# Input weights in chunks of 512 rows instead of 256, and the combined output weights made earlier in a tile that then holds the low-rank products

## The chip, the cores and the metric

The kernel runs on one core of one Trainium2 chip. The metric is device time in microseconds, the median of several runs. A difference under about 0.2% (4 us) is not told from no difference.

## What is computed

One step of one layer of a hybrid decoder, in float32: 1024 prompt rows with 16 learned rows ahead of them, and 32 rows of 8 sampled sequences, 2048 wide.

```python
u = h @ w_in                      # h: rms-normed rows; 2048 -> 7184 columns
sq, sk, sv, sg, gq, gk, gv, gg, ga = jnp.split(u, idx, axis=-1)
log_f = jax.nn.log_sigmoid(ga @ w_alpha + b_alpha) / GLA_TAU      # ga: 16 columns
o_sb  = stick_breaking_attention(sq, sk, sv)      # 8 heads of 128, the sampled rows with paged k and v
o_gla = gated_linear_attention(gq, gk, gv, log_f) # 4 heads, 128 keys, 256 values
mixed = jnp.concatenate([o_sb * silu(sg), rms_norm(o_gla) * silu(gg)], axis=-1)
y = x + rms_norm(mixed @ w_out)
```

## The kernel before

All matrix products are made in three passes of a fast float format: a factor is split into a high part (a cast) and a low part (what the cast lost), and high x high, high x low and low x high are summed in PSUM. `hT` holds the normed rows, transposed: 16 tiles of 128 columns, each with the high part (`hh`) and the low part (`hl`) of 1072 rows. It is made at the start: the rows come as nine tiles x0 to x8 (two halves each, `load_x`), are squared on ScalarE (L224), scaled on VectorE (L235), transposed on TensorE (L259) in three thirds of the rows, and evicted by ScalarE (L260, times `gpre`, the high part) and VectorE (L261, the low part). Meanwhile TensorE makes the first projection, v of head 0, from the tiles `wf` and `wfl` (L271 to L273). Some small constants are loaded beside it (L140 to L144); `nbal` (a row for the gated part, L141) is negated by VectorE (L142).

A projection to 128 columns is `inproj` (L278): 16 blocks of 128 weight rows, in each three groups of rows (c = 0, 1, 2) with three passes, summed in three PSUM banks `acc`; a following projection takes the same three banks, one after another. The weights come through `weight_chunk` (L176): one DMA of 256 rows x 128 columns into `wr`, a cast by ScalarE to `wh` (L183), a subtraction by VectorE to `wl` (L184). The pool `wp` has three buffers of each, and the next chunk's load, cast and subtraction wait for a buffer. There are 56 projections of 8 chunks: v, k and q of eight heads, gates 0 to 2, then four heads of gated linear attention (k, q, two v each) with gates 3 and 4, and the other gates beside the sampled rows' part and the output.

The order of the work is written by hand: TensorE's loop calls `W.beat()` after each group of six matmuls of `inproj`, and generators that were given to the Weaver run at their beats and issue work for the other engines: `z_feed` (L386) multiplies the paged keys `kp` with the sampled queries `qb` on VectorE (four operations `jk` for each of 512 pages), the loads of the cached values `vr` and their split into `V` (L487, L488), `attend`, `gate_rest` for each gate (L418), and `weight_forms` (L401). Within an engine, work runs in the order in which it was placed; `urgent()` places it ahead. SP issues nearly all DMAs.

`weight_forms` makes sums and differences of the four quarters of `w_out` for the output stage: 16 tiles `tf`, each with four loads (L407), four subtractions on VectorE (L411) and four writes to DRAM (`td`, L414). There is one buffer `tf`, so a tile's loads wait for the writes of the one before. A tile takes 4 x 4 + 12 + 4 x 4 + 4 x 4 = 60 beats, and the generator starts at beat 10. The eight heads and gates 0 to 2 have 24 beats for each projection, 640 with the low-rank product, which stands between the heads and the gates (beats 552 to 568).

The low-rank product (`low_rank`, L313) is the projection to the 16 columns `ga`; it is evicted to a tile `ga` of its own (L328 to L330) and used by `decay` (L730) for each of the four gated heads. At the end of a head, q is evicted from PSUM by ScalarE (L624) and VectorE (L625, the low part, also from PSUM).

A gate's columns are copied from PSUM by ScalarE (`gx`, L442); `gate_rest` then alternates between VectorE (L426, L429, L431, L432) and ScalarE (L427, L428, L430), with a tile `go` read back from DRAM for L432. For a gated head, `level` makes X on VectorE (L780, L781), its exponential on ScalarE (L782); k and q are evicted by ScalarE in pieces (L672 to L680).

In the output stage, tiles of `w_out` and of the combined weights go through `ring` (cast L1308, subtraction L1309, 512 columns each) to the matmuls L1471 to L1473; `raw()` gives the tiles `fr` in which the mixed rows are loaded.

## Time and profile before

| | |
|---|---|
| median of 3 runs | 2113.27 us (2111.09 to 2113.43) |
| the profiled execution | 2108.24 us, of which the span in the trace is 2106.5 us |
| TensorE busy | 2056.2 us, 12,546 matmuls, mean granted clock 0.995 |
| VectorE busy | 1569.7 us |
| ScalarE busy | 991.8 us |
| DMA | 301.96 MB, mean 143 GB/s |

All times of instructions below are those of the profiled execution, counted from the start of its span. Its end lies 1.7 us before the execution's, and the execution is 5.0 us faster than the median; a sum of changes is made against 2108.24. The rows of the waits name who waited, for whom, how long in total, how often, and the longest. In a row of the timeline the start and the length come first, then engine, line, operation, output and inputs, and in brackets how long the engine had stood and for what. In a row of the groups the busy time of the group and the mean of one in ns follow the first bar, the idle time ahead of them and its cause the second.

### The profile page before, as it was taken

The page shows a single profiled execution, that of the slowest core. Times are in us where ns is not written, and L with a number is a line of the kernel's source. Part 1 is how long each engine was busy: PE and PEld are TensorE (multiplying, and loading weights), DVE is VectorE, ACT ScalarE, POOL GpSimd, SP SyncE. Part 2 cuts the span into 40 slices and gives each one's busy share as a digit, 9 for nine tenths or more (in the row PEclk, how much of TensorE's full clock was granted, in tenths as well). Part 3 has the DMA queues.
Part 4 walks back from the last instruction along what each step waited for, and adds up shares of the span by engine and source line. Part 5 has one row for each costly group of instructions (what it writes and reads, how often), then busy time and mean ns, then how long its engine had stood idle before and what let it go on. Part 6 is the DMA issues. An engine that isn't in the chain of part 4 may idle for free.

```text
span 2106.5 us, 43298 instructions
## 1 busy us (share of the span) xinstructions
PE 2056.2 (98%) x12546; PEld 1868.4 (89%) x12546; DVE 1569.7 (75%) x6593; ACT 991.8 (47%) x2539; POOL 80.9 (4%) x298
## 2 busy tenths in 40 slices
PE   5999999999999999999999999999999999999998
PEld 4999999999999989999899898998888888777776
DVE  6368888889888889899889988877544347453576
ACT  7346555565655547423535335353444326332342
POOL 0000000100000000020000000000000000000000
PEclk9999999999999999999999999999999999999999
DMA  6234443544444353544353444434776666352485
GB/s 200 72 103 123 132 131 100 144 118 121 139 124 126 108 145 102 156 132 117 110 138 104 123 129 113 107 85 135 244 234 219 224 218 201 127 159 75 130 279 186
DMA packets 378505, 301.96 MB, mean 143 GB/s; under 512 B 50073, under 2 KB 318777, under 8 KB 378265
## 3 DMA queue, kind: packets, MB, share of 16 engines
q1 hardware_dynamic: 376072, 298.91, 48.1%
q8 instruction: 99, 1.62, 0.3%
q14 instruction: 142, 1.16, 0.2%
q10 hardware_dynamic: 2192, 0.27, 0.1%
HBM read 241.75 MB, written 57.31 MB: 142 GB/s over the span
## 4 chain that ended last, share of the span: by engine, by line
PE 84%; DMA 6%; DVE 6%; ACT 2%; issue 1%; SPq 0%; DVEq 0%; POOL 0%; ACTq 0%; POOLq 0%
PE acc_g L288 4%; PE acc_g L290 4%; PE b L1471 4%; PE acc_g L289 4%; PE b L1472 4%; PE b L1473 4%; PE acc_k L288 3%; PE acc_gv L288 3%; PE acc_k L289 3%; PE acc_q L288 3%; PE acc_k L290 3%; PE acc_gv L290 3%; PE acc_gv L289 3%; PE acc_q L289 3%; PE acc_q L290 3%; PE acc_v L288 3%
## 5 line engine op out<-in xcount | busy, mean ns | idle before, releaser
L386 DVE SCALAR_TENSOR_TENSOR jk<-kp,qb 128x128 f32<-128x128 f32 x2048 | 591.6, 289 | 38.9 <-DMA qb<-qsd 1.5
L288 PE MATMUL acc_g<-hT,wh_g 128*128 128x368 f32 (+2 forms) x768 | 251.7, 328 | 0.8 <-ACT gx L442 0.8
L290 PE MATMUL acc_g<-hT,wl_g 128*128 128x368 f32 (+2 forms) x768 | 248.4, 323 | 0.0
L289 PE MATMUL acc_g<-hT,wh_g 128*128 128x368 f32 (+2 forms) x768 | 247.9, 323 | 0.0
L1471 PE MATMUL b<-ring,f 128*128 128x512 f32 x416 | 165.7, 400 | 3.2 <-ACT b L1344 2.0
L386 DVE DVE_READ_ACCUMULATOR jk<-kp,qb 128x1 f32 x2048 | 166.9, 81 | 0.0
L1309 DVE TENSOR_TENSOR ring<-wr,ring 128x512 fp32r<-128x512 f32 x104 | 70.6, 690 | 128.7 <-ACT ring L1308 128.3
L1472 PE MATMUL b<-ring,f 128*128 128x512 f32 x416 | 162.8, 391 | 0.7 <-DVE ring L1309 0.5
L1473 PE MATMUL b<-ring,f 128*128 128x512 f32 x416 | 162.4, 390 | 0.0
L288 PEld LDWEIGHTS acc_g<-hT,wh_g 128*128 128x128 f32 x768 | 145.1, 189 | 12.4 <-issue 10.2
L290 PEld LDWEIGHTS acc_g<-hT,wl_g 128*128 128x128 f32 x768 | 144.9, 189 | 2.0 <-issue 2.0
L289 PEld LDWEIGHTS acc_g<-hT,wh_g 128*128 128x128 f32 x768 | 145.1, 189 | 0.7
L1308 ACT CAST ring<-wr 128x512 fp32r<-128x512 f32 x104 | 64.4, 622 | 159.0 <-DMA wr<-in_w_out_dram 80.6
L288 PE MATMUL acc_gv<-hT,wh_gv 128*128 128x384 f32 (+1 forms) x384 | 129.6, 338 | 0.0
L288 PE MATMUL acc_k<-hT,wh_k 128*128 128x378 f32 (+1 forms) x384 | 127.8, 333 | 0.0
L288 PE MATMUL acc_q<-hT,wh_q 128*128 128x368 f32 (+2 forms) x384 | 125.5, 327 | 0.0
L289 PE MATMUL acc_k<-hT,wh_k 128*128 128x378 f32 (+1 forms) x384 | 125.5, 327 | 0.0
L290 PE MATMUL acc_k<-hT,wl_k 128*128 128x378 f32 (+1 forms) x384 | 125.3, 326 | 0.0
L290 PE MATMUL acc_gv<-hT,wl_gv 128*128 128x384 f32 (+1 forms) x384 | 125.2, 326 | 0.0
L289 PE MATMUL acc_gv<-hT,wh_gv 128*128 128x384 f32 (+1 forms) x384 | 124.6, 325 | 0.0
L289 PE MATMUL acc_q<-hT,wh_q 128*128 128x368 f32 (+2 forms) x384 | 123.8, 322 | 0.0
L290 PE MATMUL acc_q<-hT,wl_q 128*128 128x368 f32 (+2 forms) x384 | 123.6, 322 | 0.0
(441 smaller groups left out, 5398.3 us busy)
## 6 DMA issues: line engine op xcount, KB each, us to landing
kp<-in_cache_k_dram SPq DMA_DIRECT2D x512, 64.0 KB
vr<-in_cache_v_dram SPq DMA_DIRECT2D x64, 512.0 KB
tf<-in_w_out_dram SPq DMA_DIRECT2D x64, 256.0 KB
qb<-qsd SPq DMA_DIRECT2D x64, 256.0 KB
td<-tf SPq DMA_DIRECT2D x64, 256.0 KB
wr_g<-in_w_in_dram SPq DMA_DIRECT2D x128, 128.0 KB
wr<-td SPq DMA_DIRECT2D x64, 256.0 KB
wr<-in_w_out_dram SPq DMA_DIRECT2D x48, 256.0 KB
```

Source lines behind the costliest of these rows:

```text
L288: mm(acc[c][:, :n], wh[:, k2, :], hh[k][:, lo:hi], start=(k == 0), stop=False)
L289: mm(acc[c][:, :n], wh[:, k2, :], hl[k][:, lo:hi], start=False, stop=False)
L290: W.mark = mm(acc[c][:, :n], wl[:, k2, :], hh[k][:, lo:hi], start=False, stop=(k == NK - 1)).ins
L386: ins = vec.scalar_tensor_tensor(jk[:], kp[:], 1.0, qbs[h, b][:, t, :], ALU.mult, ALU.mult, accum_out=zt[:, t, NPG - 1 - i:NPG - i])
L1308: act.copy(wh, r)
L1309: vec.tensor_tensor(wl, r, wh.bitcast(F32), ALU.subtract)
L1471: mm(bk[:], ah, wh, start=first and k == 0, stop=False, skip_group_check=True)
L1472: mm(bk[:], ah, wl, start=False, stop=False, skip_group_check=True)
L1473: mm(bk[:], al, wh, start=False, stop=last and k == 7, skip_group_check=True)
```

## The change

- A weight chunk is 512 rows (four blocks of 128, one DMA of 256 KB), in two buffers instead of three: 224 loads, casts and subtractions instead of 448. The first projection's own tiles hold three chunks (12 blocks in `wf`, six pairs in `wfl`), the fourth uses the pool.
- `weight_forms` pauses half as long: 2 beats between its steps and 8 behind the loads, 32 beats for a tile instead of 60. It now ends at beat 522 instead of 970.
- The tile of the low-rank products is no longer one of its own. When `weight_forms` has ended, it takes the buffer `tf` under the name `ga`; `low_rank` runs beats until it is there (beat 522 lies ahead of its 552).
- The tiles `fr` of the output stage come from another pool, `op`, which is opened later and lies where the weights lay.

```diff
-    wp_cm = tc.tile_pool(name="wp", bufs=3, side="right")
+    wp_cm = tc.tile_pool(name="wp", bufs=2, side="right")
...
     def weight_chunk(w, kk, c0, nm, dst=None):
         with urgent():
-            raw = wp.tile([P, 2, P], F32, tag="wr", name=f"wr_{nm}")
-            nc.sync.dma_start(raw[:], w[kk * 256:(kk + 1) * 256, c0:c0 + P].rearrange("(k p) c -> p k c", p=P))
+            raw = wp.tile([P, 4, P], F32, tag="wr", name=f"wr_{nm}")
+            nc.sync.dma_start(raw[:], w[kk * 512:(kk + 1) * 512, c0:c0 + P].rearrange("(k p) c -> p k c", p=P))
+            wh, wl = dst or [wp.tile([P, 4, P], F32R, tag=t, name=f"{t}_{nm}") for t in ("wh", "wl")]
...
-        wf = xp.tile([P, 14, P], F32R, tag="wf", bufs=1, name="wf")
+        wf = xp.tile([P, 12, P], F32R, tag="wf", bufs=1, name="wf")
...
         for kk in range(NK // 2):
-            wh, wl = weight_chunk(w_in[0], kk, c0, f"{nm}_{kk}")
+            if kk % 2 == 0:
+                ws = weight_chunk(w_in[0], kk // 2, c0, f"{nm}_{kk // 2}")
...
-    ga = dk.tile([96, T], F32R, tag="ga", bufs=1, name="ga")
...
+        while not ga:
+            W.beat()
+        g = ga[0]
...
                 spread(nc.sync.dma_start(t[:, i, :], w_out[0, r0:r0 + P, c0:c0 + 512]))
-                yield 4
-            yield 12
+                yield 2
+            yield 8
             for i, a, b in ((0, 1, 0), (1, 1, 2), (2, 2, 0), (3, 3, 2)):
                 spread(vec.tensor_tensor(t[:, i, :], t[:, a, :], t[:, b, :], ALU.subtract))
-                yield 4
+                yield 2
             for j, i in enumerate((0, 2, 1, 3)):
                 spread(nc.sync.dma_start(td[j][:, k, q * 512:(q + 1) * 512], t[:, i, :]))
-                yield 4
+                yield 2
+        ga.append(dk.tile([96, T], F32R, tag="tf", bufs=1, name="ga"))
...
-            return oy.tile([P, 512], F32, tag="fr", name=nm)
+            return op.tile([P, 512], F32, tag="fr", bufs=4, name=nm)
```

What this does to the order shows at three places. In the rows, a name's last number only tells tiles apart; line numbers of the changed kernel are up to 8 higher.

**The start.** SP's loads from x3 on (the two halves of x3 are `x_0_232` and `x_1_233` before, `x_0_218` and `x_1_219` now; the next two are x4's). Before:

```order
L211 DMA x_0_232<-in_x_prompt_dram 128x1024
L179 DMA wr_v_1_202<-in_w_in_dram 128x2x128
L179 DMA wr_v_2_206<-in_w_in_dram 128x2x128
L211 DMA x_1_233<-in_x_prompt_dram 128x1024
L211 DMA x_0_236<-in_x_prompt_dram 128x1024
L179 DMA wr_v_3_210<-in_w_in_dram 128x2x128
```

and now:

```order
L214 DMA x_0_218<-in_x_prompt_dram 128x1024
L179 DMA wr_v_1_202<-in_w_in_dram 128x4x128
L214 DMA x_1_219<-in_x_prompt_dram 128x1024
L214 DMA x_0_222<-in_x_prompt_dram 128x1024
L179 DMA wr_v_2_207<-in_w_in_dram 128x4x128
L179 DMA wr_v_3_212<-in_w_in_dram 128x4x128
```

The second half of x3 stood behind two loads of weights after the first, and now stands behind one; it was the fourteenth DMA of the program, counting ScalarE's, and is now the thirteenth, with x4's first half as the fourteenth. Further down SP issued the constants behind the last rows and two chunks for head 0's k. Before:

```order
L179 DMA wr_k_1_917<-in_w_in_dram 128x2x128
L179 DMA wr_k_2_941<-in_w_in_dram 128x2x128
L140 DMA biasb<-in_sb_bias_dram 128x8
L211 DMA x_0_496<-in_x_prompt_dram 128x1024
L211 DMA x_1_497<-in_x_prompt_dram 128x1024
L209 DMA x_0_500<-in_x_sample_dram 32x1024 x2
L179 DMA wr_k_3_989<-in_w_in_dram 128x2x128
L179 DMA wr_k_4_1015<-in_w_in_dram 128x2x128
L141 DMA nbal<-in_b_alpha_dram 128x4x1
L143 DMA gnrm<-in_gla_norm_g_dram 128x2x1
```

and now:

```order
L214 DMA x_1_479<-in_x_prompt_dram 128x1024
L179 DMA wr_k_1_920<-in_w_in_dram 128x4x128
L179 DMA wr_k_2_989<-in_w_in_dram 128x4x128
L140 DMA biasb<-in_sb_bias_dram 128x8
L141 DMA nbal<-in_b_alpha_dram 128x4x1
L143 DMA gnrm<-in_gla_norm_g_dram 128x2x1
L214 DMA x_0_482<-in_x_prompt_dram 128x1024
L214 DMA x_1_483<-in_x_prompt_dram 128x1024
L212 DMA x_0_486<-in_x_sample_dram 32x1024 x2
```

`nbal` and `gnrm` have moved ahead of x7 (`x_0_496` before, `x_0_482` now) and x8. On VectorE the negation of `nbal` (L142) stood between x6's sums and the first hT of the second third. Before:

```order
L235 TENSOR_SCALAR x_0_373<-x_0_373,r_x_403 128x1024
L235 TENSOR_SCALAR x_1_374<-x_1_374,r_x_403 128x1024
L226 TENSOR_REDUCE sq_529<-ssq_524 128x1
L161 TENSOR_SCALAR v_x_531<-sq_529 128x1
L142 TENSOR_SCALAR nbal<-nbal 128x4
L261 SCALAR_TENSOR_TENSOR hT_146<-tx_0_506,gpre,hT_146 128x384
L261 SCALAR_TENSOR_TENSOR hT_147<-tx_1_512,gpre,hT_147 128x384
```

and now:

```order
L238 TENSOR_SCALAR x_0_222<-x_0_222,r_x_330 128x1024
L238 TENSOR_SCALAR x_1_223<-x_1_223,r_x_330 128x1024
L229 TENSOR_REDUCE sq_386<-ssq_381 128x1
L264 SCALAR_TENSOR_TENSOR hT_157<-tx_11_400,gpre,hT_157 128x384
L142 TENSOR_SCALAR nbal<-nbal 128x4
L161 TENSOR_SCALAR v_x_388<-sq_386 128x1
L264 SCALAR_TENSOR_TENSOR hT_158<-tx_12_406,gpre,hT_158 128x384
L264 SCALAR_TENSOR_TENSOR hT_159<-tx_13_412,gpre,hT_159 128x384
```

It has moved to behind the twelfth hT of the first third, ahead of x5's sums (x4 is `x_0_222` here, and x5's scaling comes later).

**The end of a head.** VectorE around the eviction of q (L625 before, L633 now) of head 1. Before:

```order
L488 TENSOR_TENSOR V_1_3136<-vr_1_3184,V_1_3135 127x384
L184 TENSOR_TENSOR wl_v_1_3235<-wr_v_1_3232,wh_v_1_3234 128x256
L386 SCALAR_TENSOR_TENSOR jk_0_6_2_3079,zt_0_2824<-kp_0_6_2866,qb_0_2543 128x128
L488 TENSOR_TENSOR V_1_3136<-vr_2_3224,V_1_3135 127x256
L625 SCALAR_TENSOR_TENSOR q_1_2578<-acc_q_0_2580,q_1_2577 128x368
L386 SCALAR_TENSOR_TENSOR jk_0_6_3_3081,zt_0_2824<-kp_0_6_2866,qb_0_2543 128x128
L488 TENSOR_TENSOR V_1_3136<-vr_2_3224,V_1_3135 33x128
L625 SCALAR_TENSOR_TENSOR q_1_2578<-acc_q_1_2581,q_1_2577 128x384
L184 TENSOR_TENSOR wl_v_2_3303<-wr_v_2_3300,wh_v_2_3302 128x256
L625 SCALAR_TENSOR_TENSOR q_1_2578<-acc_q_2_2582,q_1_2577 128x272
```

and now:

```order
L496 TENSOR_TENSOR V_1_3021<-vr_1_3069,V_1_3020 127x384
L393 SCALAR_TENSOR_TENSOR jk_0_6_2_2971,zt_0_2726<-kp_0_6_2763,qb_0_2448 128x128
L393 SCALAR_TENSOR_TENSOR jk_0_6_3_2973,zt_0_2726<-kp_0_6_2763,qb_0_2448 128x128
L633 SCALAR_TENSOR_TENSOR q_1_2484<-acc_q_0_2486,q_1_2483 128x368
L393 SCALAR_TENSOR_TENSOR jk_0_7_0_3002,zt_0_2726<-kp_0_7_2804,qb_0_2448 128x128
L496 TENSOR_TENSOR V_1_3021<-vr_2_3109,V_1_3020 127x256
L393 SCALAR_TENSOR_TENSOR jk_0_7_1_3004,zt_0_2726<-kp_0_7_2804,qb_0_2448 128x128
L633 SCALAR_TENSOR_TENSOR q_1_2484<-acc_q_1_2487,q_1_2483 128x384
L393 SCALAR_TENSOR_TENSOR jk_0_7_2_3006,zt_0_2726<-kp_0_7_2804,qb_0_2448 128x128
L183 TENSOR_TENSOR wl_v_1_3183<-wr_v_1_3180,wh_v_1_3182 128x512
L633 SCALAR_TENSOR_TENSOR q_1_2484<-acc_q_2_2488,q_1_2483 128x272
```

One jk more stands between the first and second eviction of q, one between the second and the third, and the split of the weights ahead of the third is 512 wide instead of 256.

**Gate 2, ahead of the first gated head.** VectorE ahead of gate 2's first step (L426 before, L434 now). Before:

```order
L386 SCALAR_TENSOR_TENSOR jk_4_1_3_15887,zt_4_15843<-kp_4_1_15689,qb_4_15656 128x128
L386 SCALAR_TENSOR_TENSOR jk_4_2_0_15912,zt_4_15843<-kp_4_2_15726,qb_4_15656 128x128
L386 SCALAR_TENSOR_TENSOR jk_4_2_1_15914,zt_4_15843<-kp_4_2_15726,qb_4_15656 128x128
L184 TENSOR_TENSOR wl_gk_1_16102<-wr_gk_1_16099,wh_gk_1_16101 128x256
L386 SCALAR_TENSOR_TENSOR jk_4_2_2_15916,zt_4_15843<-kp_4_2_15726,qb_4_15656 128x128
L411 TENSOR_TENSOR tf_0_15350<-tf_0_15350 128x512
L386 SCALAR_TENSOR_TENSOR jk_4_2_3_15918,zt_4_15843<-kp_4_2_15726,qb_4_15656 128x128
L426 TENSOR_SCALAR gs_16_15937<-gx_0_15932 128x368
```

and now:

```order
L393 SCALAR_TENSOR_TENSOR jk_4_1_1_15324,zt_4_15284<-kp_4_1_15142,qb_4_15109 128x128
L393 SCALAR_TENSOR_TENSOR jk_4_1_2_15326,zt_4_15284<-kp_4_1_15142,qb_4_15109 128x128
L393 SCALAR_TENSOR_TENSOR jk_4_1_3_15328,zt_4_15284<-kp_4_1_15142,qb_4_15109 128x128
L393 SCALAR_TENSOR_TENSOR jk_4_2_0_15353,zt_4_15284<-kp_4_2_15173,qb_4_15109 128x128
L393 SCALAR_TENSOR_TENSOR jk_4_2_1_15355,zt_4_15284<-kp_4_2_15173,qb_4_15109 128x128
L393 SCALAR_TENSOR_TENSOR jk_4_2_2_15357,zt_4_15284<-kp_4_2_15173,qb_4_15109 128x128
L393 SCALAR_TENSOR_TENSOR jk_4_2_3_15359,zt_4_15284<-kp_4_2_15173,qb_4_15109 128x128
L434 TENSOR_SCALAR gs_16_15371<-gx_0_15367 128x368
```

The subtraction of the combined weights (L411) and a split of 256 have gone from here.

More of the change, by code (lines that the diff above doesn't have):

```diff
@@ L241, in hybrid_step @@
                 constants()
-                for kk in range(NK // 2):
-                    dst = (wf[:, 2 * kk:2 * kk + 2, :], wfl[kk]) if kk < 7 else None
-                    wchunks.append(weight_chunk(w_in[0], kk, C_SV, f"v0_{kk}", dst))
+                for kk in range(NK // 4):
+                    dst = (wf[:, 4 * kk:4 * kk + 4, :], wfl[2 * kk:2 * kk + 2]) if kk < 3 else None
+                    wchunks.extend(weight_chunk(w_in[0], kk, C_SV, f"v0_{kk}", dst))
         for i in range(3):
@@ L269, in hybrid_step @@
             for k in range(NK):
-                wh, wl = (t[:, k % 2, :] for t in wchunks[k // 2])
+                wh, wl = wchunks[k]
                 mm(o_, wh, hh[k][:, lo:hi], start=(k == 0), stop=False)
@@ L285, in inproj @@
                 n = hi - lo
-                for k2 in range(2):
-                    k = 2 * kk + k2
-                    mm(acc[c][:, :n], wh[:, k2, :], hh[k][:, lo:hi], start=(k == 0), stop=False)
-                    mm(acc[c][:, :n], wh[:, k2, :], hl[k][:, lo:hi], start=False, stop=False)
-                    W.mark = mm(acc[c][:, :n], wl[:, k2, :], hh[k][:, lo:hi], start=False, stop=(k == NK - 1)).ins
+                for k in (2 * kk, 2 * kk + 1):
+                    wh, wl = ws[k % 4]
+                    mm(acc[c][:, :n], wh, hh[k][:, lo:hi], start=(k == 0), stop=False)
+                    mm(acc[c][:, :n], wh, hl[k][:, lo:hi], start=False, stop=False)
+                    W.mark = mm(acc[c][:, :n], wl, hh[k][:, lo:hi], start=False, stop=(k == NK - 1)).ins
                 if kk == NK // 2 - 1:
@@ L345, in page_dma @@
         done.append(d.ins)
+    ga = []
     heads_ready = []
@@ L729, in decay @@
                 ps = gps.tile([P, 512], F32, tag="P", bufs=2, name=f"al{g}_{c}")
-                mm(ps[:, :n], wal[:], ga[:, lo:hi], start=True, stop=True)
+                mm(ps[:, :n], wal[:], ga[0][:, lo:hi], start=True, stop=True)
                 ny = stage(f"ny{g}_{c}")[:, :n]
@@ L1200, in hybrid_step @@
         oy = out.enter_context(tc.tile_pool(name="oy", bufs=4))
-        for tag in ("wr", "fr"):
-            oy.tile([P, 512], F32, tag=tag, name=f"{tag}_")
+        oy.tile([P, 512], F32, tag="wr", name="wr_")
         def ytile(nm):
```

18 lines of the change are left out of this document (10 added, 8 removed).

## The prediction

> **What bounds the kernel now.** I read the page first: its busy rows and the chain of work that ended last.
>
> ```profile
> PE 2056.2 (98%) x12546; PEld 1868.4 (89%) x12546; DVE 1569.7 (75%) x6593; ACT 991.8 (47%) x2539; POOL 80.9 (4%) x298
> PE 84%; DMA 6%; DVE 6%; ACT 2%; issue 1%; SPq 0%; DVEq 0%; POOL 0%; ACTq 0%; POOLq 0%
> ```
>
> TensorE is the bound. The change takes no matmul away, so it can only fill TensorE's holes or tear new ones. The span of this execution is 2106.5 us, of which TensorE is busy 2056.2; its own time is 2108.24, which is 5.03 below the median of the runs shown (2113.27). The second view is the list of TensorE's waits; the largest, and those the change can touch, are these.
>
> ```profile
> PE tx L259 <- DVE x L235: 16.2, 3, 13.2
> PE tx L259 <- DVE hT L261: 3.1, 2, 2.9
> PE acc_gq L288 <- ACT gk L673: 2.2, 1, 2.2
> PE acc_gk L288 <- ACT gx L442: 1.8, 1, 1.8
> PE acc_ga L321 <- DVE q L625: 1.3, 1, 1.3
> PE acc_gq L288 <- ACT gk L680: 1.2, 1, 1.2
> ```
>
> No row of that list says that a matmul waited for a weight of `inproj` (wh from L183, wl from L184): larger chunks cannot win there. The third view is the table of windows. It shows the heads to be full, and what a hole does to the granted clock (the PEclk column, behind POOL's).
>
> ```profile
> 100.00:700.00 600.00, 599.78 (x3655) 575.88 (x3654) 506.99 (x2369) 337.56 (x867) 48.18 (x170) 1.00 0.45 124
> 40.80:43.70 2.90, 0.00 (x0) 0.00 (x0) 0.73 (x3) 1.55 (x5) 0.00 (x0) 0.75 0.05 2
> 43.70:48.00 4.30, 4.29 (x18) 4.04 (x19) 4.26 (x12) 3.35 (x10) 0.00 (x0) 0.50 0.00 0
> 48.00:52.00 4.00, 4.00 (x25) 3.87 (x25) 3.86 (x13) 3.92 (x16) 0.00 (x0) 0.87 0.00 0
> 908.60:912.00 3.40, 3.40 (x12) 3.06 (x12) 3.40 (x17) 0.48 (x3) 0.00 (x0) 0.59 0.35 103
> ```
>
> In the heads VectorE has 507 of 600 us of work: 93 us are free. After the hole at 40.8 the clock is 0.50 for 4.3 us and 0.87 for 4 us, which loses 4.3 x 0.50 + 4 x 0.13 = 2.7 us of matmul time beside the 2.9 us of the hole.
>
> **Term 1, splitting the weights: 0.** The rows below have both shapes.
>
> ```profile
> L183 ACT CAST wh_g<-wr_g 128x256 fp32r<-128x256 f32 x128 | 51.4, 402 | 125.1 <-PE acc_g L289 102.5 <-issue 17.1 <-DMA kp<-in_cache_k_dram 2.4
> L184 DVE TENSOR_TENSOR wl_g<-wr_g,wh_g 128x256 fp32r<-128x256 f32 x128 | 53.9, 421 | 86.1 <-ACT wh_g L183 85.8
> L411 DVE TENSOR_TENSOR tf<-tf 128x512 f32<-128x512 f32 x64 | 43.9, 686 | 0.0
> L1308 ACT CAST ring<-wr 128x512 fp32r<-128x512 f32 x104 | 64.4, 622 | 159.0 <-DMA wr<-in_w_out_dram 80.6 <-PE b L1473 44.4 <-DMA wr<-td 31.0
> L1309 DVE TENSOR_TENSOR ring<-wr,ring 128x512 fp32r<-128x512 f32 x104 | 70.6, 690 | 128.7 <-ACT ring L1308 128.3
> ```
>
> 448 casts of 402 ns become 224 of 622: 180 - 139 = 41 us less on ScalarE. 448 subtractions of 421 ns become 224 of 690: 189 - 155 = 34 us less on VectorE. All of it lies beside the matmuls. The cover holds: a buffer of two is released one chunk ahead of its use, one of three two half chunks ahead, the same time; the split of one chunk takes 0.62 + 0.69 instead of 0.40 + 0.42 us, so a weight has 0.5 us less to spare. If the cover fails, a late weight costs that much each time. Bounds 0 to +1.
>
> **Term 2, the start: -4.5.** Up to 44 us TensorE follows the normalised input.
>
> ```profile
> SPq L211 <- DMA gpre<-in_norm_pre_g_dram: 6.9, 1, 6.9
> 20.12 1.06 ACT L224 ACTIVATE hT<-x 128x1024 fp32r<-128x1024 f32 x1 [2.91 <-DMA x<-in_x_prompt_dram]
> 21.79 0.68 PE L271 MATMUL acc_v<-hT,wf 128*128 128x378 f32 x1 [1.61 <-ACT hT L260]
> 33.65 0.79 ACT L183 CAST wh_k<-wr_k 128x256 fp32r<-128x256 f32 x2 [0.62 <-DMA wr_k<-in_w_in_dram]
> 29.63 0.61 SPq L140 DMA_DIRECT2D biasb<-in_sb_bias_dram  x1
> 36.30 0.37 SPq L141 DMA_DIRECT2D nbal<-in_b_alpha_dram x1
> 38.52 0.37 SPq L143 DMA_DIRECT2D gnrm<-in_gla_norm_g_dram x1
> 42.97 0.17 DVE L142 TENSOR_SCALAR nbal<-nbal 128x4 f32<-128x4 f32 x1 [2.77 <-DMA nbal<-in_b_alpha_dram]
> 43.71 0.90 PE L259 MATMUL tx<-ident,x 128*128 128x128 f32 x3 [2.93 <-DVE hT L261]
> ```
>
> SP stood 6.9 us for the load of `gpre` with x3's second half behind it; ScalarE then idled 2.91 us for that half. The order now puts this half ahead of the stall and x4 behind it, so ScalarE begins some 2 us earlier. It soon gives about half back: the splits of the third and fourth chunk and of head 0's first k chunk now stand ahead of the third, fourth and seventh hT, for loads that are no earlier. The wait of 0.62 for wr_k ahead of the twelfth hT goes. `nbal` is issued right behind `biasb` (at 29.63 before) instead of at 36.30, but VectorE's wait for it moves up too, to behind the twelfth hT of the first third, with the other four hT and the scaling of x5 queued behind it, for which TensorE waits. It took 42.97 - 36.30 = 6.7 us from issue to use; behind a shorter or equal queue it is there at 34 to 36.5, while VectorE comes to it at 32.5 to 33.5. So a stall of 1 to 3 us stands there in place of 2.77 later, and VectorE leaves it at 34 to 36.5, where it worked on the thirteenth hT at 35.6 before. What I take: 1.1 us from the earlier first third, 2.8 from the later stall that is gone, 2.7 of clock won and 2.1 of clock lost behind the new hole: -4.5. `gnrm` ahead of x7 costs SP 38.52 - 36.30 = 2.2 us, hidden, since x7 is needed past 40. Bounds: +1 (nbal at 38 or later) and -7 (no stall).
>
> A rule speaks against the clock's part. The Trainium skill (TensorE: Matmul & The Clock Gate, Part 1: The HAM clock gate) has the clock fall only after an idle window of about 3.4 us; by it no hole here costs more than itself, and this term would be -3.9. The trace differs: 0.50 after 2.9 us, 0.59 after 2.2 us.
>
> **Term 3, the gates and the first GLA head: -1.8.** The combined weights took 60 beats for each of 16 tiles, to beat 970; now 32, to beat 522 of the 640 that the heads and first gates have. Their subtractions leave this place.
>
> ```profile
> L411 DVE TENSOR_TENSOR tf<-tf x4: 686/688/709, 881.2 to 897.0; 128x512 f32<-128x512 f32 x4
> 882.44 0.51 ACT L427 ACTIVATE gs<-gs 128x368 f32<-128x368 f32 x1 [3.23 <-DVE gs L426]
> 888.40 0.54 DVE L432 TENSOR_TENSOR gs<-gs,go 128x368 f32<-128x368 f32 x1 [1.80 <-DMA go<-od]
> 908.52 0.45 PE L288 MATMUL acc_gq<-hT,wh_gq 128*128 128x384 f32 x1 [2.16 <-ACT gk L673]
> 911.82 1.06 ACT L782 ACTIVATE X<-X 128x1024 f32<-128x1024 f32 x1 [2.92 <-DVE X L781]
> 913.35 0.41 PE L288 MATMUL acc_gq<-hT,wh_gq 128*128 128x304 f32 x1 [1.19 <-ACT gk L680]
> ```
>
> ScalarE waited 3.23 us for VectorE's L426, with the eviction behind it that TensorE wanted (1.76 us). One of the four subtractions stood just ahead of L426: 0.6 us earlier. The other three lie between the DMA wait of L432 (to 888.40) and the work that holds ScalarE until 911.82, with merged splits: 3 x 0.6 + 0.3 = 2.1 us. The hole of 2.2 us goes, but the third gk eviction still waits for X at L782, so TensorE starts at 906.4, is through two banks at 908.4 (twelve matmuls, 3.40 us at 0.59, are 2.0 at full clock) and stands there until 913.35 - 2.1 = 911.2, 2.8 us instead of 1.19. The clock then falls past the last wait, where its loss counts (it was hidden ahead of 913.35 before). -0.6 - 2.1 + 0.9 (half of a loss of 1.8, between 3.40 x 0.41 = 1.4 here and 2.7 at the start; half, as I don't know whether the hole splits) = -1.8. By the skill's rule the 0.9 would go: -2.7. Bounds 0 and -4.5.
>
> **Term 4, the end of each head: +0.9.** Weight forms now press their work into the heads: 64 x 0.69 = 44 us, 5.9 per head instead of 3.2, of 93 us free. On the whole it fits. SP's loads of the next tile now stand 2 beats behind the last write of the one before, not 4, and wait for it to land; kp is loaded six pages ahead, so nothing behind them is late. The narrow place is where q leaves PSUM by VectorE and the next head's matmuls take its three banks in turn.
>
> ```profile
> L386 DVE SCALAR_TENSOR_TENSOR jk<-kp,qb 128x128 f32<-128x128 f32 x2048 | 591.6, 289 | 38.9 <-DMA qb<-qsd 1.5
> 215.11 0.53 DVE L625 SCALAR_TENSOR_TENSOR q<-acc_q,q 128x368 fp32r<-128x368 f32 x1
> 215.97 0.54 DVE L625 SCALAR_TENSOR_TENSOR q<-acc_q,q 128x384 fp32r<-128x384 f32 x1
> 216.44 0.41 DVE L184 TENSOR_TENSOR wl_v<-wr_v,wh_v 128x256 fp32r<-128x256 f32 x1
> 216.77 0.42 DVE L625 SCALAR_TENSOR_TENSOR q<-acc_q,q 128x272 fp32r<-128x272 f32 x1
> 216.94 0.34 PE L288 MATMUL acc_v<-hT,wh_v 128*128 128x378 f32 x1
> 218.08 0.39 PE L288 MATMUL acc_v<-hT,wh_v 128*128 128x316 f32 x1
> ```
>
> The second bank is free at 216.51 and taken at 216.94, the third at 217.19 and 218.08: 0.43 and 0.89 us to spare. Now a jk more stands ahead of the second (0.29), and two more in all and a split of 0.69 instead of 0.42 ahead of the third (0.29 + 0.29 + 0.27 = 0.85): no margin is left there. I take 0.13 us in each of seven heads; bounds 0 and +3 (0.4 each).
>
> **Term 5, the rest: -0.6.** Head 7 has no combined weights beside it now; its 1.3 us wait for q may go or stay: -0.6, bounds 0 and -1.3. The low-rank products wait for their tile, which is free 30 beats before they need it: 0. `fr` comes from the pool that follows the weights': its first tiles wait for the last wh and wl, released before the output stage: 0, bounds -1 and +1.
>
> **The sum.** 0 - 4.5 - 1.8 + 0.9 - 0.6 = -6.0: 2108.24 becomes 2102.2; with the 5.03 by which the runs lie higher, **2107.3**.
>
> **Rivals.**
> *Nothing on the path changes.* nbal comes at 37 or later, the stall only moves, and the gk eviction eats what VectorE gives. For it: both end at waits that the change doesn't remove. Against: x3's 2.91 us and four subtractions do go. Time: 2111 to 2114.
> *VectorE late at the head ends, slower.* If one tf subtraction more (0.6) and a backlog of one page's jk (4 x 0.29 = 1.2) stand ahead of q's last eviction, TensorE stands 1.8 us at each of eight head ends, and the clock may take up to 1.5 more: 14 to 26 us, less 6.9 won elsewhere: 2121 to 2133. It decides as soon as VectorE reaches q's first eviction more than 0.4 us late, the margin of the second bank; two of the heads now have a tf subtraction right ahead of it. Against: 93 us are free in 600.
> *Only a new order, no gain from merging:* if a 512-wide split doesn't pay (a cast above 0.80 us), ScalarE and VectorE gain nothing; still term 2 and most of term 3: 2108 to 2110.
>
> **How the numbers follow.** Forecast 0.57 (2100 to 2111 alone), nothing changes 0.20, VectorE late 0.18, no merging gain 0.05. The range reaches from 2099 (terms 2 and 3 near their ends) to 2119, which leaves out the slower rival and little else. A measurement can tell about 0.2%, 4.2 us, from no change: faster means below 2109.0. Nine tenths of the forecast and half of the last case lie there, the second case lies within: faster 0.51 + 0.03 = 0.54, same 0.28, slower 0.18.
>
> **What would show it.** Right: ScalarE's wait for x3 gone; the wait for nbal at L142 near 33 to 36 and no hole at 40.8; the clock 1.00 there; no wait at gk L673; TensorE at 599 or more in 100 to 700. Wrong: a row "acc <- DVE q" or a wait for wl or wh among TensorE's waits with several times to it, or the casts of 128x512 above 0.8 us.

## The result and the profile after

The changed kernel takes 2099.55 us (median of 6 runs, 2097.17 to 2101.63), beside 2113.35 for the kernel before on the same chip (6 runs, 2110.91 to 2116.59). The ratio is 0.9943, 95% interval 0.9932 to 0.9954: 0.57% faster. The forecast was 2107.3 in a range from 2099 to 2119. The direction held and the range held the time, barely; the size did not. The two profiled executions, 2108.24 before and 2099.06 after, differ by 9.2 us, the medians by 13.8. Both differences want an explanation.

The busy row of the changed kernel's page:

```profile
PE 2053.5 (98%) x12546; PEld 1865.4 (89%) x12546; DVE 1561.0 (74%) x6372; ACT 962.4 (46%) x2315; POOL 81.2 (4%) x298
```

ScalarE has 224 instructions less and VectorE 221 (three chunks of the first projection are subtracted in two parts), and TensorE is the bound as before. From TensorE's waits in the changed kernel:

```profile
PE tx L262 <- DVE x L238: 3.8, 2, 3.1
PE acc_v L292 <- DVE q L633: 2.7, 3, 1.5
PE acc_gq L292 <- ACT gk L681: 2.6, 1, 2.6
...
PE acc_gq L292 <- ACT gk L688: 0.8, 1, 0.8
...
PE Cs L1105 <- PE acc_g L294: 0.8, 1, 0.8
```

Gone are the waits for `hT` L261 (2.9 at once), of the gk product for `gx` L442 (1.8) and of the low-rank product for q (1.3). The wait of the gq product for the eviction of gk (2.6) is still there. New is the second row: TensorE waits for the eviction of q, three times. That is the sign that the prediction had named as wrong, and the windows show it:

```profile
100.00:700.00 600.00, 596.06 (x3618) 570.06 (x3618) 512.09 (x2300) 330.35 (x785) 47.07 (x168) 1.00 0.52 146
700.00:800.00 100.00, 100.00 (x613) 90.88 (x612) 87.16 (x405) 58.35 (x140) 8.22 (x31) 1.00 0.43 115
1400.00:1500.00 100.00, 98.29 (x650) 89.84 (x649) 70.62 (x328) 44.97 (x118) 3.45 (x14) 1.00 0.57 172
```

In the heads TensorE was busy 599.78 of 600 us before and is now busy 596.06: the heads, full before, have got holes. Elsewhere it gained. The last two of these windows, in the kernel before:

```profile
1400.00:1500.00 100.00, 96.12 (x628) 88.85 (x630) 73.06 (x354) 47.06 (x134) 3.37 (x14) 0.98 0.52 153
700.00:800.00 100.00, 98.70 (x604) 89.82 (x603) 86.97 (x408) 58.74 (x149) 7.77 (x29) 1.00 0.44 118
```

The granted clock differs too. Ahead of TensorE's end it stood at 0.50 in three stretches before, 42.2 to 49.1, 909.2 to 912.6 and 1479.2 to 1482.6 us, and now stands there in one, 909.0 to 912.4. That is 10.3 us less at half clock; an estimate from these lengths is that at most about 5 of the 9.2 us come from it.

A way to add such windows up: TensorE runs the same projections in the same order in all kernels here, so I took from each trace the start of the first matmul of a projection and subtracted that of the profile before. Negative is ahead. The places are the first projection behind the start (at 73.9 us before), q of head 7 (744.6), the first gate (794.6), q of the first GLA head (908.5), the first gate behind the four GLA heads (1385.6), the fourth one, in the samples' part (1485.4), the first matmul of the output (1758.9) and the end of TensorE's work (2096.9). Each row is one profiled execution. The names of the runs are those of the next section.

| | start | head 7 | gate | GLA q | behind GLA | samples | output | end |
|---|---|---|---|---|---|---|---|---|
| after | -2.9 | +3.0 | +1.6 | -0.2 | -3.0 | -6.6 | -8.1 | -9.2 |
| e1, new pace, 256 rows | -1.1 | +4.5 | +3.0 | +3.0 | +3.2 | +1.9 | +1.2 | +0.7 |
| e2, splits in halves | -2.2 | +1.0 | -0.3 | -0.2 | +1.3 | -1.3 | -1.9 | -0.5 |
| e3, V's loads first | -2.9 | -1.4 | -2.8 | -5.1 | -7.8 | -11.0 | -11.9 | -12.4 |
| e4, like before | +0.3 | +0.3 | +0.3 | +1.4 | +2.8 | +3.0 | +3.6 | +6.5 |
| e5, subtractions in halves | -2.6 | +2.0 | +0.6 | -0.6 | -0.3 | -3.2 | -4.1 | -0.3 |
| e6, casts in halves | -3.2 | +2.3 | +0.9 | -1.0 | -3.6 | -5.2 | -6.8 | -5.9 |
| e7, loads in halves | -0.1 | +12.0 | +10.7 | +9.8 | +7.1 | +2.5 | +2.4 | +3.4 |
| e8, V first, nbal on GpSimd | -4.3 | -2.9 | -4.2 | -6.9 | -8.0 | -12.1 | -13.5 | -14.0 |
| e9, before, nbal on GpSimd | -1.3 | -1.2 | +1.0 | +2.0 | +3.7 | +5.5 | +5.6 | +6.4 |
| e10, 256 rows, four buffers | -0.4 | +10.6 | +9.1 | +9.0 | +9.7 | +6.6 | +6.3 | +8.4 |
| e11, e1 with V first | -0.2 | +1.7 | +0.2 | -0.1 | -0.1 | -1.3 | -0.6 | -2.4 |

So the change won 2.9 us at the start, lost 5.9 in the heads, won 1.4 + 1.9 in head 7, the gates and the first GLA head's k, 2.8 in the other GLA heads, 3.6 in the samples' part, 1.5 on to the output and 1.1 in it. The row of e4 is a warning for single executions: its engines did nearly what they did before, and it ends 6.5 us late. All of that arises behind the first gate: e4 and e9, whose order behind the start is that of before, move by about 0.1 us from "start" to "head 7", and in the GLA heads alone lose 1.4 and 1.8. So the losses in the heads are read safely from one execution, and a difference of 1 or 2 us in a later part is not.

The loss in the heads can be followed at the end of head 1. ScalarE's rows of the changed kernel:

```profile
215.75 0.60 ACT L495 CAST V<-vr 127x256 fp32r<-127x256 f32 x2 [2.47 <-DMA vr<-out_dram]
216.26 0.48 ACT L632 ACTIVATE q<-acc_q 128x384 fp32r<-128x384 f32 x1
216.64 0.60 ACT L182 CAST wh_v<-wr_v 128x512 fp32r<-128x512 f32 x1
217.15 0.39 ACT L632 ACTIVATE q<-acc_q 128x272 fp32r<-128x272 f32 x1
```

Then VectorE's, in the same microseconds:

```profile
216.19 0.42 DVE L496 TENSOR_TENSOR V<-vr,V 127x256 fp32r<-127x256 f32 x1 [1.50 <-ACT V L495]
...
216.77 0.56 DVE L633 SCALAR_TENSOR_TENSOR q<-acc_q,q 128x384 fp32r<-128x384 f32 x1
```

ScalarE stands 2.47 us for the load of `vr`, the rows from which `V` of the next head is split, and the eviction of q (L632) is queued behind; VectorE stands 1.50 for the same split with its part of the eviction (L633) behind it. From 100 to 745 us ScalarE waits 10.2 us in all for `vr`, and 4.2 before. The load is late because SP issued it late. Before, all three loads were out by 199.4 us:

```profile
L482 SPq DMA_DIRECT2D vr<-out_dram x3: 405/425/438, 197.1 to 199.4; - x3
```

In the changed kernel the last of them goes out 13 us later, behind loads of the combined weights (`tf`) and of cached keys (`kp`) that wait for their buffers:

```profile
202.77 1.01 SPq L414 DMA_DIRECT2D tf<-in_w_out_dram  x1
203.97 1.52 SPq L350 DMA_DIRECT2D kp<-in_cache_k_dram  x2
206.31 0.34 SPq L414 DMA_DIRECT2D tf<-in_w_out_dram  x1
206.89 1.31 SPq L350 DMA_DIRECT2D kp<-in_cache_k_dram  x1
209.98 0.40 SPq L490 DMA_DIRECT2D vr<-out_dram  x1
...
212.89 0.40 SPq L490 DMA_DIRECT2D vr<-out_dram  x1
```

### The profile page after: what moved, and what is told of

It is laid out like the page before. It is cut to its first block, busy times and chain, and to the rows that moved or that the text cites. A ratio compares the mean times of both kernels' runs of the same rounds, so it can differ in the third digit from the quotient of the medians.

```text
span 2097.3 us, 42175 instructions
## 1 busy us (share of the span) xinstructions
PE 2053.5 (98%) x12546; PEld 1865.4 (89%) x12546; DVE 1561.0 (74%) x6372; ACT 962.4 (46%) x2315; POOL 81.2 (4%) x298
## 4 chain that ended last, share of the span: by engine, by line
PE 85%; DVE 7%; DMA 4%; ACT 2%; issue 2%; SPq 0%; DVEq 0%; ACTq 0%; POOL 0%
PE acc_g L292 6%; PE acc_g L293 6%; PE acc_g L294 6%; PE b L1478 4%; PE b L1479 4%; PE b L1480 4%; PE acc_k L292 3%; PE acc_k L293 3%; PE acc_k L294 3%; PE acc_q L292 3%; PE acc_v L292 3%; PE acc_q L293 3%; PE acc_q L294 3%; PE acc_v L294 3%; PE acc_v L293 3%; PE acc_gv L292 2%
## 5 line engine op out<-in xcount | busy, mean ns | idle before, releaser
L292 PEld LDWEIGHTS acc_g<-hT,wh_g 128*128 128x128 f32 x768 | 144.3, 188 | 12.3 <-issue 10.6
```

Source lines behind the costliest of these rows:

```text
L292: mm(acc[c][:, :n], wh, hh[k][:, lo:hi], start=(k == 0), stop=False)
```

## The experiments

My theory from the two traces: the new pace of the combined weights costs the heads 6 us through V's late loads, and what wins elsewhere is that ScalarE, VectorE and SP have fewer instructions for the weights. Its rivals: the earlier combined weights win by themselves, and merging is worth nothing, since no matmul waits for a weight. Each run stood beside runs of the kernel before on its chip; the ratio to those is given with its interval.

**The pace alone (e1).** The kernel before, with the shorter pauses and the low-rank products in the combined weights' tile; chunks stay at 256 rows.

```diff
...
-                yield 4
-            yield 12
+                yield 2
+            yield 8
...
+        ga.append(dk.tile([96, T], F32R, tag="tf", bufs=1, name="ga"))
```

> The kernel before with the faster pace of the combined weights and the low-rank products in their tile, but with weight chunks of 256 rows in three buffers. Theory A (the pace takes the combined weights out of the gated part and puts them in the way of the V loads in the heads): the start as before, 0; the heads 5 to 7 us longer; head 7, gate 2 and the gated heads 5 to 6 us shorter; the rest 0: about 2112 to 2115. Theory B (all the gain of the change comes from the chunks): nothing comes back after the heads, 2117 to 2121.

Measured: 2112.5 us (12 runs, 2108.96 to 2119.79), ratio 1.0005 [0.9996, 1.0015]. The pace by itself wins nothing. It takes 5.6 us from the heads, by the same new wait:

```profile
PE acc_gq L288 <- ACT gk L677: 3.4, 1, 3.4
PE acc_v L288 <- DVE q L629: 3.4, 2, 1.8
```

Head 7 and the first gate then give back 1.5 us; the gk wait, from which term 3 was to win, has grown from 2.2 to 3.4. The time and the heads are theory A's, but of the 5 to 6 us that it expected back only 1.3 have come by the end of the GLA heads.

**The splits in halves (e2).** The changed kernel, each chunk of 512 rows cast and subtracted in two halves of 256 elements.

```diff
-                act.copy(wh[:], raw[:])
-                vec.tensor_tensor(wl[:], raw[:], wh[:].bitcast(F32), ALU.subtract)
+                for i in (slice(0, 2), slice(2, 4)):
+                    act.copy(wh[:, i], raw[:, i])
+                    vec.tensor_tensor(wl[:, i], raw[:, i], wh[:, i].bitcast(F32), ALU.subtract)
...
```

> The changed kernel with its loads of 512 rows in two buffers, but each chunk split in two casts and two subtractions of 256 as before, so the 41 us on ScalarE and 34 us on VectorE are not saved. Theory A (fewer loads on SP and another order pay, engine time does not): within 2 us of the changed kernel, 2098 to 2102. Theory B (the engine time saved is the gain): 5 to 10 us slower than the changed kernel, 2105 to 2110.

Measured: 2105.94 (8 runs, 2104.61 to 2108.32), 0.9969 [0.9959, 0.998]: 6.4 us above the changed kernel, as theory B had it. Merging the splits pays, although no matmul waits for a weight.

**The halves apart (e5, e6).** Only the subtraction in halves, then only the cast.

```diff
-                vec.tensor_tensor(wl[:], raw[:], wh[:].bitcast(F32), ALU.subtract)
+                for i in (slice(0, 2), slice(2, 4)): vec.tensor_tensor(wl[:, i], raw[:, i], wh[:, i].bitcast(F32), ALU.subtract)
```

> The changed kernel, with only VectorE's subtraction of each 512-row chunk made in two halves (two 128x256 instructions); the cast stays one 128x512 instruction on ScalarE. Halving both had cost 6.4 us (2105.94 against 2099.55). Theory V (the merged subtraction pays, because VectorE is the engine that runs late in the gates and the first GLA heads and holds the evictions that TensorE waits for): most of it returns here, 2103.5 to 2106.5, and the offset of TensorE between the end of the heads and the end of the first GLA head is about 3 us worse than in the changed kernel. Theory S (the merged cast on ScalarE pays): 2099 to 2101.

```diff
-                act.copy(wh[:], raw[:])
+                for i in (slice(0, 2), slice(2, 4)): act.copy(wh[:, i], raw[:, i])
...
```

> The changed kernel, with only ScalarE's cast of each chunk made in two halves of 256 elements; the subtraction stays one 128x512 instruction on VectorE. Theory V: 2099 to 2101.5. Theory S: 2103.5 to 2106.5, with the waits for gk and q evictions on ScalarE longer. If each half is worth about half: both runs at 2102 to 2103.

Measured: 2107.99 (8 runs, 2103.36 to 2112.03), 0.9978 [0.9966, 0.9991], and 2103.11 (5 runs, 2102.36 to 2107.57), 0.9963 [0.995, 0.9977]. They are 8.4 and 3.6 us over the changed kernel, together more than the 6.4 of both at once. The first lies above what either theory gave; the second lies between theory V's 2099 to 2101.5 and theory S's 2103.5 to 2106.5. The table shows where the sum goes wrong: in e5, 4.9 us of the difference arise behind the first output matmul (-4.1 to -0.3, where the changed kernel goes from -8.1 to -9.2), where the edit changes nothing. Up to that matmul the losses are 4.0 for the subtraction, 1.4 for the cast and 6.2 for both, which nearly add up. The subtraction's loss sits in the GLA heads: between "GLA q" and "behind GLA" the changed kernel wins 2.8, e5 loses 0.3 and e2 loses 1.5, and e6 wins 2.6. A part of this is the granted clock: behind the waits for gk it stands at 0.50 for 6.8 us in e5 and in e2, for 3.4 in the changed kernel, and not at all in e6. By TensorE's holes alone, from 860 to 1390 us, e5 has 6.5 us, e2 6.1, e6 5.0 and the changed kernel 4.3. So VectorE's part is the larger, as theory V had it, and about in the place that it named, by one execution of each. In e5's output TensorE stands for 6.8 us instead of 3.6, and its clock is at 0.50 from 2011.9 to 2015.3; what moves that part is not settled by these runs.

**The loads in halves (e7).** The changed kernel, each chunk loaded by two DMAs of 256 rows into its one tile; the splits stay merged.

```diff
-            nc.sync.dma_start(raw[:], w[kk * 512:(kk + 1) * 512, c0:c0 + P].rearrange("(k p) c -> p k c", p=P))
+            for r0 in (0, 256): nc.sync.dma_start(raw[:, r0 // P:r0 // P + 2], w[kk * 512 + r0:kk * 512 + r0 + 256, c0:c0 + P].rearrange("(k p) c -> p k c", p=P))
```

> The changed kernel, with each 512-row chunk loaded by two DMAs of 256 rows into the one tile, so that SP issues as many weight loads as before the change; the merged cast and subtraction stay. Theory L (SP's shorter row of issues is what made the samples and the output part about 6 us faster, since their loads are issued earlier): the offset won behind the last GLA head falls from 6 to 2 or less, and the time is 2103 to 2106. Rival (the engines' merged instructions and freed order made it, not SP): 2099 to 2101.5, the part behind the GLA heads as in the changed kernel.

Measured: 2111.78 (11 runs, 2105.65 to 2116.5), 0.9995 [0.9983, 1.0008]. With as many weight loads as before, the whole gain is gone: 12.2 us. But the theory had the wrong place. The samples' part keeps its gain (4.6 us from "behind GLA" to "samples"); what is lost are 2.8 us at the start, 6.2 in the heads and, less surely by one execution, 3.5 behind the samples.

```profile
PE acc_v L292 <- DVE q L633: 6.2, 4, 2.5
PE tx L262 <- DVE x L238: 5.7, 2, 5.0
```

The first row is the same wait as in the changed kernel, 2.7 there. SP issues in order, and now twice as many weight loads stand ahead of `vr`: from 100 to 745 us ScalarE waits 19.5 us for `vr`, 10.2 in the changed kernel. At the end of head 2 the last part of `vr` holds ScalarE for 3.4 us with the eviction of q behind it, where the changed kernel does not wait at all. The second is the start: x's rows go out behind more loads (3.8 in the changed kernel).

**Everything but the chunks' size (e10).** 256 rows in four buffers, which hold the rows of two buffers of 512; pace, low-rank tile and `fr` as in the changed kernel.

```diff
-    wp_cm = tc.tile_pool(name="wp", bufs=3, side="right")
+    wp_cm = tc.tile_pool(name="wp", bufs=4, side="right")
...
```

> The whole change except the chunks' size: 256 rows in four buffers (the same rows held as two of 512), the combined weights at the new pace, the low-rank products in their tile, the output part's tiles placed as in the changed kernel. Theory L (what the change won is the fewer and coarser weight loads, casts and subtractions): 2109 to 2113, the heads losing 5 us or more, the part behind the GLA heads winning 2.5 us or less as in the run with three buffers. Rival (the longer look-ahead in rows is what wins behind the GLA heads): that part wins 5 to 6 us, 2105 to 2108.

Measured: 2111.84 (12 runs, 2108.33 to 2118.72), 1.0002 [0.999, 1.0013]. The total is theory L's; the part behind the GLA heads wins 3.4 us up to the first output matmul, more than e1's 2.0 and less than the changed kernel's 5.1. So a longer look-ahead may carry some of it, which one execution of each does not settle. The heads lose 11.0 us, 5.4 more than in e1. That is not a later `vr`: ScalarE waits 16.7 us for it, 16.3 in e1. Of the 5.4, 3.4 are the granted clock, which stands at 0.50 for 3.4 us behind each of two holes in e10's heads (last section) and is full in e1's.

**V's loads first (e3, e11).** The three loads of `vr` are placed as urgent, ahead of the combined weights' and the cached keys': in the changed kernel, and in e1.

```diff
-                nc.sync.dma_start(sv[1:KT + 1, :nt], src[c * 378:c * 378 + nt * KT].rearrange("(a p) d -> p a d", p=KT))
+                with urgent():
+                    nc.sync.dma_start(sv[1:KT + 1, :nt], src[c * 378:c * 378 + nt * KT].rearrange("(a p) d -> p a d", p=KT))
...
```

> The changed kernel with the loads of V placed as urgent, so that they stand ahead of the combined weights' loads on SP again. Theory A (the heads lost time because ScalarE waits for V with the eviction of q behind it): the waits for q by TensorE of 2.7 us go, the heads gain 3 to 4.5 us: 2095 to 2097. Theory B (VectorE is late at the head ends by its own work): unchanged, 2098 to 2101.

Measured: 2098.85 (6 runs, 2095.85 to 2100.41), 0.9936 [0.9924, 0.9949]. The wait for q has left the list, ScalarE waits 4.3 us for `vr` instead of 10.2, and the heads lose 1.5 us instead of 5.9: the mechanism in the heads is theory A's, and shown. The time is in theory B's range. Of the 4.4 us the end of the trace keeps 3.2 and the medians 0.7; the profiled execution was the fastest of the six, so by times alone e3 is not told from the changed kernel.

> The kernel before with the new pace and the low-rank products in the combined weights' tile (chunks of 256 rows in three buffers, 2112.5 when run so), and the loads of V's cached rows put first among SP's issues. Theory (the new pace costs the heads 5.6 us only because it puts V's loads behind the combined weights' and the cached K's): the heads lose 0 to 2 us, 2107 to 2110. Rival (with 256-row chunks another part of the pace, VectorE's subtractions close together, holds the evictions): the heads lose 4 us or more, 2111 to 2114.

Measured: 2108.06 (12 runs, 2104.83 to 2110.91), 0.9984 [0.9975, 0.9993], 4.4 us under e1. The heads lose 1.9 us instead of 5.6, and ScalarE waits 3.6 us for `vr` instead of 16.3. The pace costs the heads their time through V's loads, with chunks of either size.

**The negation of `nbal` (e4, e9, e8).** e4 has the line that negates it moved to behind the heads' set-up, in the kernel before.

```diff
-        vec.tensor_scalar(nbal[:], nbal[:], -1.0, None, ALU.mult)
...
         a = w_alpha[0]
+        vec.tensor_scalar(nbal[:], nbal[:], -1.0, None, ALU.mult)
```

> The kernel before with the negation of nbal moved from the start to the low-rank weights' place, some 600 us later; nothing else. Theory A (the wait of 2.77 us and the clock behind it are what the start loses): the hole at 40.8 us goes, with its clock, 3 to 5 us faster than before, 2108 to 2110. Theory B (TensorE catches up by 74 us in any case, since it is behind in transposes): 0 to 1 us, 2112 to 2114.

Measured: 2114.46 (12 runs, 2106.63 to 2120.05), 1.0007 [0.9995, 1.002]. This says nothing on the theory, since the instruction stood early on VectorE all the same and waited as before:

```profile
44.20 0.17 DVE L302 TENSOR_SCALAR nbal<-nbal 128x4 f32<-128x4 f32 x1 [3.15 <-DMA nbal<-in_b_alpha_dram]
```

e9 gives it to GpSimd instead, in the kernel before; nothing else moves on TensorE, ScalarE or SP.

```diff
-        vec.tensor_scalar(nbal[:], nbal[:], -1.0, None, ALU.mult)
+        pool.tensor_scalar(nbal[:], nbal[:], -1.0, None, ALU.mult)
```

> The kernel before, with the negation of the bias made on GpSimd in place of VectorE; TensorE's, ScalarE's and SP's instructions stand in the same order as before. Theory (VectorE's wait for that load opens the hole of 3.3 us in TensorE at 41 us, and nothing else is late there): TensorE is ahead by 2 to 4 us by the end of the first head, the time 2109 to 2111. Rival (the x tiles and first weights, issued late by SP, end at the same time behind it): ahead by less than 1 us, 2112 to 2114.

Measured: 2111.38 (12 runs, 2105.23 to 2115.05), 0.9995 [0.9985, 1.0006]. The hole of 2.9 us is gone (the 3.3 of the expectation is e4's), and TensorE is ahead by only 1.3 us behind the start: between the two expectations. The granted clock fell at the start all the same, to 0.50 from 37.8 to 41.2 us, where before it did from 42.2 to 49.1.

e8 does the same in the changed kernel, together with V's loads first.

> The changed kernel, with the three loads of V's cached rows put first among SP's issues (as in the run of that alone, 2098.85) and the negation of the bias made on GpSimd, so that VectorE never waits for that load. Theory (the negation still costs VectorE 0.5 us and TensorE about 1 us at the start, and the late V cost 4.4 us in the heads): 2095 to 2098. Rival (what the heads win is given back in the gates and the GLA part, where a later wait ends at the same time): 2098 to 2100, as the run with V's loads alone.

Measured: 2094.24 (5 runs, 2092.64 to 2096.59), 0.9917 [0.9904, 0.9931], just under the expected 2095 to 2098, and the fastest of all; its slowest run lies under the changed kernel's fastest. The negation is again worth 1.4 us at the start, V's loads 4.5 in the heads. What stays on TensorE's list are these:

```profile
PE acc_gq L292 <- ACT gk L689: 2.1, 1, 2.1
PE b L1479 <- ACT b L1352: 2.0, 2, 1.0
PE acc_gq L292 <- ACT gk L682: 1.9, 1, 1.9
```

The prices of the parts do not add up. Splits in halves cost 6.4 us and loads in halves 12.2, but the changed kernel lies only 12.9 under e1, which has neither merged. So what each is worth depends on the other, and no share of the gain can be given to one.

## Why the prediction was right, and where it was not

The sign was right, but not by the sum's own reckoning: two of its terms held in their mechanism, one was short by 5 us, and gains of 9 us stood in no term.

**The offset of 5.03.** The sum was made against the profiled execution, and the distance of that execution from the median was added. By the medians the sum is short by the whole 7.75 us for which the forecast was high: -13.8 measured for -6.0. The two profiled executions, in which the terms are measured below, show 3.2 of this, -9.2 for -6.0. The other 4.6 do not show there, since the execution before lay 5.1 us under its median and the one after 0.5 under. A single execution is a draw: the 13 profiled ones on record lie from 5.1 us under to 4.8 us over the median of their kernel, and of 78 runs of the kernel before one alone is faster than 2108.24. How executions of nearly the same work differ is to be seen in e9, whose TensorE, ScalarE and SP do in the same order what they did before, in an execution of 2114.64:

```profile
PE acc_gq L288 <- ACT gk L673: 2.9, 1, 2.9
PE Cs L1097 <- issue: 2.8, 1, 2.8
...
PE acc_ga L321 <- DVE q L625: 1.9, 1, 1.9
PE acc_gk L288 <- ACT gx L442: 1.9, 1, 1.9
PE acc_gq L288 <- ACT gk L680: 1.6, 1, 1.6
```

They are the holes of before (2.2, 2.3, 1.3, 1.8, 1.2), each longer by 0.1 to 0.7. More of it is the granted clock: from 75 us to TensorE's end it stands at 0.50 for 20.5 us in e9 and for 6.8 before. The changed kernel has closed the third and fourth of the holes and shortened the second to 0.8. Its mean granted clock is 0.9975 over its six runs, that of the kernel before 0.9951 over 72. Of 2113 us the difference is 5 us, an estimate of how much of the 13.8 between the medians is clock. No run tried this by itself.

**Term 1, 0.** This is the step that failed most. The splits were costed as hidden "beside the matmuls", since no matmul waits for a weight. That is so, and e2 shows that they are worth 6 us all the same: they stand on ScalarE's and VectorE's queues ahead of evictions for which TensorE does wait, in the GLA heads above all. The halved count of loads stood in no term: half as many on SP (e7) are worth 12.2 us under the new pace, 9 of them at the start and in the heads.

**Term 2, -4.5, measured -2.9.** The hole at 40.8 is gone and the clock is 1.00, as forecast. VectorE's wait for `nbal` came at the place and time forecast, only shorter (row of the timeline):

```profile
36.20 0.17 DVE L142 TENSOR_SCALAR nbal<-nbal 128x4 f32<-128x4 f32 x1 [0.47 <-DMA nbal<-in_b_alpha_dram]
```

x3 also came 2 us earlier, as these rows of ScalarE show (20.12 and a wait of 2.91 before):

```profile
17.98 1.06 ACT L227 ACTIVATE hT<-x 128x1024 fp32r<-128x1024 f32 x1 [0.33 <-DMA x<-in_x_prompt_dram]
...
22.60 0.62 ACT L185 CAST wf<-wr_v 128x512 fp32r<-128x512 f32 x1 [1.45 <-DMA wr_v<-in_w_in_dram]
```

TensorE's holes between 13 and 74 us shrank from 9.4 to 7.5 us, which leaves 1.0 for the clock. It is full all along now, so by the forecast's price of 2.7 for the clock behind the hole it should have given the whole 2.7; that price was too high, and the 2.1 for a clock lost behind the new stall did not come due. The 1.1 us of an earlier first third did not come, since the scaling of the third row tile is later (a wait of 3.1 instead of 2.2) and ScalarE stands 1.45 us for the third chunk.

**Term 3, -1.8, measured -1.9; the mechanism fell.** The hole at gk's first eviction was to go; it is 2.6 us, longer than before. The four subtractions did leave, and in e1, where they leave too, this place wins nothing (+3.0 to +3.0). Why gk's eviction came no earlier is to be seen in what ScalarE does just ahead of it, before and after:

```profile
906.79 0.46 ACT L735 ACTIVATE e<-e 128x304 f32<-128x304 f32 x1 [5.20 <-issue]
906.86 0.46 ACT L743 ACTIVATE e<-e 128x304 f32<-128x304 f32 x1 [4.90 <-POOL lv L714]
```

This is a step of `decay` whose input VectorE makes one line earlier (L734, L742 now); VectorE began that at 906.20 us before and at 906.47 now. The 2.8 us of the four subtractions went into 0.9 us more of waiting for `go` (2.71 instead of 1.80) and into four more `jk` in the same stretch (40 instead of 36). So the wait that the sum should have followed is the one for `decay`, and it stands in no term. What the change won here is mostly the wait at `gx`, 1.8 us where the sum had 0.6, less 0.5 by which the wait for gk grew.

**Term 4, +0.9, measured +5.9.** The loss at q's last eviction came as computed: between two places of trouble each head end costs 0.1 to 0.2 us (TensorE's lag goes from 0.71 to 0.86 to 1.02 us across the ends of heads 2 and 3). The sentence that failed is "kp is loaded six pages ahead, so nothing behind them is late": `vr` stands behind them, and e3 shows that it carries 4.4 of the 5.9. Of the 1.5 that e3 still loses, 0.8 lie in head 1, ahead of its k. The slower rival had the right wait ("acc <- DVE q") and the wrong frequency: two or three head ends, not eight.

**Term 5, -0.6, measured -1.4** for head 7: the wait of 1.3 for q went whole. The gains of 2.8 + 3.6 + 1.5 + 1.1 us from the GLA heads to the end were in no term. The last two are no larger than what e4 and e9 differ from before in such parts (up to 2.9 us); the one in the samples' part recurs in e3, e7 and e8. There SP's rows show one reason, before first, then after:

```profile
1465.02 0.38 SPq L179 DMA_DIRECT2D wr_g<-in_w_in_dram  x1
...
1468.13 0.38 SPq L179 DMA_DIRECT2D wr_g<-in_w_in_dram  x1
1468.61 0.42 SPq L391 DMA_DIRECT2D zd<-zt  x1
...
1471.04 0.38 SPq L179 DMA_DIRECT2D wr_g<-in_w_in_dram  x1
1471.47 0.46 SPq L1114 DMA_DIRECT2D dz<-zd  x1
```

```profile
1461.83 0.39 SPq L179 DMA_DIRECT2D wr_g<-in_w_in_dram  x1
...
1463.99 0.32 SPq L398 DMA_DIRECT2D zd<-zt  x1
...
1465.84 0.42 SPq L1122 DMA_DIRECT2D dz<-zd  x1
```

A weight load waits on SP until a buffer is free, and everything behind it waits too. Before, three such loads stand in the 6.5 us ahead of `dz`; now one does. `dz`, the samples' input, goes out 5.6 us earlier, of which 3.6 is TensorE's own lead by then (1456.9 before). In e7 both halves of a chunk share one buffer and so one wait. Over the gate around `dz` (1456.9 to 1485.4 before) the changed kernel wins 3.0 us, e7 2.9, and e1 none; TensorE's wait at `Cs` is 0.8 instead of 2.3, and the granted clock, at 0.50 from 1479.2 to 1482.6 before, stays full. That the fewer places at which SP can stand make it is argued from these rows; no run took that wait away alone.

The forecast's chance for the case that happened (0.54 for faster) thus rested in part on terms that came out otherwise, and that the kernel came out faster was in part luck: the two that were right in mechanism, 2 and the head 7 part of 5, give -4.3, and the heads take more than that back. Without the merged splits and loads the time is e1's: no change.

## What to carry to other kernels

Cost an instruction that nothing waits for by what is queued behind it: half as many loads on an in-order queue was worth 12 us here though no matmul ever waited for one of them, because loads behind them (x at the start, V's rows in the heads) were wanted soon. When background work is paced faster, list for each in-order queue which urgent transfer it now precedes, and place that one first; doing so here won back about 4 us of the heads in two kernels, though in one of them the time did not show it. And take one profiled execution for one draw: here such a draw lay up to 5 us from the median of its kernel, so a sum made against it is good to no better than that.

## What the runs showed of the hardware

The granted clock does not follow from the length of a hole alone. The windows behind holes, in e10 and then in e7: in e10 it fell behind a hole of 2.4 us (216.0 to 218.4) and one of 1.9 (594.2 to 596.1):

```profile
219.00:223.00 4.00, 4.00 (x19) 3.86 (x18) 3.38 (x17) 0.73 (x3) 0.00 (x0) 0.59 0.25 65
...
598.00:603.00 5.00, 5.00 (x26) 4.54 (x25) 4.00 (x23) 1.25 (x7) 0.75 (x1) 0.68 0.32 78
```

In both it stood at 0.50 for 3.4 us, 218.9 to 222.3 and 597.8 to 601.2, with TensorE busy all the while, which costs 1.7 us each. In e7 it stayed full behind holes of 1.7 us (216.7 to 218.4) and of 2.5 (312.2 to 314.7):

```profile
219.00:223.00 4.00, 3.86 (x25) 3.52 (x24) 4.00 (x21) 1.45 (x6) 0.08 (x1) 1.00 0.33 83
...
316.00:321.00 5.00, 5.00 (x35) 4.56 (x34) 4.79 (x28) 1.23 (x6) 0.20 (x1) 1.00 0.56 175
```

So a hole of about 2 us sometimes costs up to twice its length and sometimes only itself. The Trainium skill (TensorE: Matmul & The Clock Gate, Part 1: The HAM clock gate) has the clock fall after an idle window of about 3.4 us that runs freely, whatever the kernel does. The stretches of 3.4 us, and that length alone does not decide, agree with these traces; that it takes a whole idle window does not, since none of these holes is that long.
